# Gated-recurrence values and gates for two heads at a time, in a hybrid decoder block on one core

## The chip, the cores and the metric

The kernel runs on one core of a Trainium2 chip. The metric is the device time of the core in microseconds (us). Three runs of the kernel before gave 1631.12, 1628.74 and 1627.1 us, so the median is 1628.74 us.

Engine names: PE is the matrix engine (PEld its weight loads), DVE the vector engine, ACT the scalar engine, POOL the GpSimd engine, SP the engine whose queue issues most DMAs. Each engine takes its instructions in the order in which the program lists them, and waits where a semaphore holds the next one back.

## The reference, cut to what matters

One decoder block: x is (1, 1024, 1024) float32. A gated linear recurrence with four heads (HGRN2) and a sparse attention with eight heads are merged by gates; a squared-ReLU MLP of width 4096 follows.

```python
xn = rmsnorm(h, norm1_g)
proj = xn @ w_in
a_q, a_f, a_i, a_g, b_q, b_kv, b_gate, m_gate = split(proj)     # a_*: 4 heads x 128
y_a = hgrn2_mixer(a_q, a_f, a_i, a_g, lb, hgrn_norm_g)          # a_i: values, a_g: output gate
y_b = nsa_mixer(rope(b_q), ...)                                 # kc, vc: compressed keys and values
g_a, g_b = split(sigmoid(m_gate))
h = h + (g_a * (y_a @ w_br_a) + g_b * (y_b @ w_br_b)) @ w_out
hn = rmsnorm(h, norm2_g)
h = h + square(relu(hn @ w_ff1)) @ w_ff2
return rmsnorm(h, final_g)

# in hgrn2_mixer, by chunks of 64 tokens, for each head:
f = lb + (1 - lb) * sigmoid(f_pre); b = cumsum(log f)
o = tril(q e^b (k e^-b)^T) v + (q e^b) S                        # S: state ahead of the chunk
S = e^(b_last) S + (k e^(b_last - b))^T v
o = rmsnorm(o, norm_g) * silu(g)

# in nsa_mixer: compressed keys (and values alike)
blocks = tok[:, blk_idx] + pe                                   # 63 blocks of 32 tokens
kc = gelu(flatten(blocks) @ w1) @ w2                            # w1: 2048 x 256, w2: 256 x 64
```

## The kernel before

**Products.** A float32 product is made from three matmuls (`mm3`, lines 241 to 244): each operand is split into a rounded part (`whi`, `xh`) and a rest (`wlo`, `xl`). Weights come through a stream `W` (class `Stream`, line 119): SP loads a tile `wraw` of 512 KB, ACT casts it to `whi` (line 152), and DVE, or POOL for every third tile, subtracts to get `wlo` (line 155). The stream loads a set number of tiles ahead of use and splits fewer; the order of its entries is fixed by the `add_...` calls at lines 170 to 216.

**What sets the order.** The program is written out by hand, with generators for work that runs beside the main line. `spawn` starts a generator, `pump(ns)` in the main line advances a clock by `ns` and lets a generator whose due time has come take its next piece, and `drain` runs a generator to its end on the spot, with nothing of the main line between its pieces. A `yield 5000.0` in a generator asks for a pause of 5000 ns by that clock.

**Main line, in order.**

- To 44 us: `proj_vg(0)`: x comes in, is normalised, transposed (`pt`, `xh`, `xl`), and the values and gates of head 0 are made in 128x256 matmuls (`pv`).
- 44 to 290 us: `proj_f`, `proj_q` (tiles `gT`, 128x512 matmuls) and `proj_vg` for heads 1 to 3; the recurrence of the head before (`hgrn(h)`, line 451) runs beside them. It works in two halves, each with state updates on DVE (`S`, lines 507 to 512), outputs `po`, a normalisation (ACT, POOL, DVE, `h` at line 534) and transposes `py` (line 540).
- To about 400 us: gates `m` and the branch product `z` (`pz`), and the 280-column product for keys, values and the attention's gates (`pp`).
- 400 to about 548 us: the eight gate tiles of branch B (`gT`, written to `gb_d`) and `proj_b(0)` (`pp`, `kvt`, `qt`), with `compress()` (line 621) beside them. For each of k and v, compress has tokens transposed (`ptk`, `tokS`), four sets of `fh` (8 ACT and 8 DVE instructions each, lines 657 and 658), 12 matmuls `ph` on each set with a tile of its own weight stream `C`, a gelu chain on `ct` (lines 670 to 678), transposes `pgl` (line 685), and a last small product `pc2`.
- 548 to about 900 us: `proj_b(1)` and attention; then merge and `w_out` to 992 us (`po`, `hx` at line 1408).
- From 992 us: the MLP. `norm2` (line 1116) normalises the rows of `hx`, the sums `hs` and `hn` are transposed (`pt`, line 1108), split (`xoh`, `xol`, line 1114) and used in the first MLP matmuls `f1a`. The MLP's weights are split into `w1op` by `f1_prep` (line 1200) through `split2` (line 1191). A generator-like helper `ahead` runs the next such splits.

Of the kernel before, what the change touches and what calls it, by code (L numbers as in the profile page):

```python
# [10 lines left out]
F32R = mybir.dt.float32r  # L11
# [9 lines left out]
NT = T // 128  # L21
# [33 lines left out]
def tile_hybrid_block(ctx, tc, x, positions, norm1_g, w_in, lb_param, hgrn_norm_g, pe_k, pe_v,  # L55
# [116 lines left out]
    def add_vg(h):  # L172
        for i in range(2):
            W.add([vg_w[:, i * 4:(i + 1) * 4, e, h * 128:(h + 1) * 128] for e in range(2)], (4, 256))
# [17 lines left out]
    for h in range(1, 4):  # L192
        add_f(h)
        add_q(h)
        add_vg(h)
    ZSEQ = []
    for ct in range(8):
        ZSEQ.append(("m", ct))
        if ct >= 2:
            ZSEQ.append(("z", ct - 2))  # L200
    ZSEQ += [("z", 6), ("z", 7)]
    for kind, ct in ZSEQ:
        if kind == "m":
            add_mg(ct)
        elif ct % 2 == 0:
            W.add(w_cols(w_br_a[0], ct * 128, 256, k=4), (4, 256))
    for k0, k in ((0, 3), (3, 3), (6, 2)):
        W.add([w_cols(w_in2, C_KV, 256, k0=k0, k=k), w_cols(w_in2, C_BG, 24, k0=k0, k=k)], (k, 280))
    for ct in range(8):
        add_mg(8 + ct)  # L210
# [15 lines left out]
    W.ensure(2, 0)  # L226
# [78 lines left out]
    def vg_pair(h, tp, wvg, prologue=False):  # L305
        pv = psB("pv")
        for e in range(2):
            t = tp * 2 + e
            if prologue:
                if t + 4 < NT:  # L310
                    load_x(t + 4)
                if t:
                    transposed(XN.pop(t), t, XT[t // 4])
                if t + 2 < NT:
                    norm1(t + 2)
                if t in (1, 2):
                    W.ensure(W.i + t, W.i + t)
            for kt in range(KT):
                w = wvg[kt // 4]
                mm3(pv[:, e * 256:(e + 1) * 256], X_st(kt, t), (w[0][:, kt % 4, :], w[1][:, kt % 4, :]),  # L320
                    kt == 0, kt == KT - 1)
            pump(2600)
        if tp % 2 == 0:
            VG[h, tp // 2] = s4(name="vg").rearrange("p (i t c) -> p i t c", i=2, t=4)
        vg = VG[h, tp // 2]
        nc.vector.tensor_copy(vg[:, :, (tp % 2) * 2:(tp % 2) * 2 + 2, :].rearrange("p i e c -> p e i c"),
                              pv.rearrange("p (e i c) -> p e i c", e=2, i=2))

    def proj_vg(h, prologue=False):
        if prologue:  # L330
            norm1(0)
            W.ahead = 0
        wvg = [W.get(), W.get()]
        if prologue:
            transposed(XN.pop(0), 0, XT[0])
            norm1(1)
            W.ahead = 2
        for tp in range(4):
            vg_pair(h, tp, wvg, prologue)
# [11 lines left out]
    proj_vg(0, prologue=True)  # L351
# [99 lines left out]
    def hgrn(h):  # L451
        S = None
        st = []
        for q4 in range(2):
# [81 lines left out]
            yield 5000.0  # L536
# [840 lines left out]
    for th in range(2):  # L1377
# [107 lines left out]
```

## Time and profile before

| what | value |
|---|---|
| median of three runs | 1628.74 us (1627.1 to 1631.12) |
| profiled execution | 1628.69 us, its span 1626.6 us |
| PE busy | 1599.6 us |
| mean granted clock of PE | 0.998 of full speed |
| DVE, ACT, POOL busy | 67%, 46%, 36% of the span |

The profile is of one execution, and 2.1 us of its time lie around the span. Busy time of PE counts matmuls from start to a modelled end; the step from one start to the next shows the pace. The list of waits gives, for PE, each line that waited, the instruction that ended the wait, and the total. The chain of waits that ended last is 91% PE. The timeline lists instructions in order of start; in brackets stands the idle time of the engine just before the instruction, and what ended it.

### The profile page before, as it was taken

Reading aid. Unit: us, or ns where it says so; the run is one execution under the profiler, and the core shown is the slowest. Engines: PE = TensorE matmul, PEld = TensorE weight load, DVE = VectorE, ACT = ScalarE, POOL = GpSimd, SP = SyncE. Lnnn points to the kernel's source line nnn. Section 1 sums busy time; section 2 is a strip of 40 time slices with the busy share of each in tenths; the row PEclk is TensorE's granted clock in tenths of the full one; section 3 lists DMA queues with packets and bytes.
Section 4 is the critical chain, followed back from the end, with each engine's and each line's share of the span. In section 5 each row is a group of like instructions: output and inputs, shape, how many; then the busy total and the mean of one; then the engine's idle time right before and its main releaser. Section 6 shows DMA issues by size and latency. Waiting matters only on the chain.

```text
span 1626.6 us, 22947 instructions
## 1 busy us (share of the span) xinstructions
PE 1599.6 (98%) x8342; PEld 1339.9 (82%) x8342; DVE 1085.2 (67%) x1635; ACT 742.9 (46%) x1422; POOL 579.1 (36%) x567
## 2 busy tenths in 40 slices
PE   8999999999999999999999998999999999999998
PEld 7898898889888888788878877888888888888886
DVE  6464354122537466988887557988888868888766
ACT  5343335230646365877764324433333446333443
POOL 2222222010112354444341124455555303664554
PEclk9999999999999999999999999999999999999999
DMA  6211111232425000000027832344444599988852
GB/s 189 73 38 29 39 40 26 89 95 91 133 91 172 27 1 1 1 2 1 2 71 281 277 109 81 127 156 155 143 148 151 192 331 324 313 298 319 296 188 104
DMA packets 145827, 211.67 MB, mean 130 GB/s; under 512 B 11649, under 2 KB 72241, under 8 KB 145714
## 3 DMA queue, kind: packets, MB, share of 16 engines
q1 hardware_dynamic: 145714, 210.21, 38.3%
q8 instruction: 66, 1.08, 0.3%
q14 instruction: 47, 0.39, 0.1%
HBM read 164.03 MB, written 46.14 MB: 129 GB/s over the span
## 4 chain that ended last, share of the span: by engine, by line
PE 91%; DVE 3%; ACT 3%; issue 1%; DMA 1%; POOL 1%; POOLq 0%; SPq 0%; ACTq 0%; DVEq 0%
PE f1c L1226 8%; PE f1d L1226 5%; PE gT L242 5%; PE gT L244 5%; PE gT L243 5%; PE f1a L1226 5%; PE oT L1045 5%; PE sc L894 4%; PE pT L934 4%; PE gA L243 3%; PE gA L244 3%; PE gA L242 3%; PE gB L242 3%; PE gB L243 3%; PE gB L244 3%; PE pp L242 2%
## 5 line engine op out<-in xcount | busy, mean ns | idle before, releaser
L1314 POOL TENSOR_TENSOR gr<-gw 128x512 f32<-128x512 f32 x80 | 126.4, 1591 | 134.3 <-DVE gu L1195 50.7
L155 POOL TENSOR_TENSOR wlo<-wraw,whi 128x1024 fp32r<-128x1024 f32 (+1 forms) x28 | 67.4, 2407 | 273.9 <-ACT whi L152 269.6
L242 PE MATMUL gT<-xh,whi 128*128 128x512 f32 x384 | 152.6, 398 | 0.2 <-ACT xh L263 0.2
L244 PE MATMUL gT<-xh,wlo 128*128 128x512 f32 x384 | 150.3, 392 | 0.0
L243 PE MATMUL gT<-xl,whi 128*128 128x512 f32 x384 | 150.2, 391 | 0.0
L155 DVE TENSOR_TENSOR wlo<-wraw,whi 128x1024 fp32r<-128x1024 f32 (+2 forms) x59 | 81.9, 1395 | 93.5 <-ACT whi L152 89.0
L919 POOL TENSOR_SCALAR P<-P,den,gat 128x640 f32<-128x640 f32 (+7 forms) x128 | 100.1, 797 | 120.2 <-DVE den L915 61.4
L1195 DVE TENSOR_TENSOR gu<-gr,gu 128x512 fp32r<-128x512 f32 x112 | 103.0, 920 | 48.3 <-ACT gu L1194 48.1
L1194 ACT CAST gu<-gr 128x512 fp32r<-128x512 f32 x112 | 69.4, 620 | 136.9 <-DVE gx L1195 107.5
L1226 PE MATMUL f1c<-xoh,w1op 128*128 128x512 f32 x384 | 126.1, 390 | 0.0
L1195 DVE TENSOR_TENSOR gx<-gr,gx 128x512 fp32r<-128x512 f32 x112 | 111.1, 992 | 4.4 <-ACT gx L1194 4.2
L937 DVE TENSOR_TENSOR pth<-pT,pth 128x512 fp32r<-128x512 f32 (+1 forms) x148 | 98.8, 683 | 21.3 <-ACT pth L936 19.9
L910 ACT ACTIVATE P<-sc,den 128x640 f32<-128x640 f32 (+7 forms) x128 | 89.7, 705 | 43.9 <-DVE den L901 40.6
L894 PE MATMUL sc<-kS,qS 128*128 128x512 f32 (+3 forms) x384 | 96.7, 361 | 0.6 <-ACT P L910 0.5
L1045 PE MATMUL oT<-pth,vS 128*128 128x512 f32 x264 | 96.7, 441 | 0.0
L936 ACT CAST pth<-pT 128x512 fp32r<-128x512 f32 (+1 forms) x148 | 85.1, 588 | 23.9 <-PE pT L934 21.3
L901 DVE TENSOR_REDUCE den<-sc 128x1 f32<-128x640 f32 (+7 forms) x96 | 84.6, 884 | 16.7 <-PE sc L897 15.9
L152 ACT CAST whi<-wraw 128x1024 fp32r<-128x1024 f32 (+2 forms) x87 | 88.6, 1038 | 12.1 <-PE po L243 6.1
L243 PE MATMUL gA<-gx,gu 128*128 128x512 f32 x224 | 87.4, 390 | 0.4 <-DVE gx L1195 0.2
L242 PE MATMUL gA<-gx,gu 128*128 128x512 f32 x224 | 87.3, 390 | 0.0
L244 PE MATMUL gA<-gx,gu 128*128 128x512 f32 x224 | 87.2, 389 | 0.0
L242 PE MATMUL gB<-gx,gu 128*128 128x512 f32 x224 | 87.1, 389 | 0.0
(343 smaller groups left out, 4450.2 us busy)
## 6 DMA issues: line engine op xcount, KB each, us to landing
gw<-in_w_ff_dram SPq DMA_DIRECT2D x160, 256.0 KB, 5.3
gr<-u_d SPq DMA_DIRECT2D x112, 256.0 KB, 5.2
wraw<-in_w_in_dram SPq DMA_DIRECT2D x40, 512.0 KB, 5.1
w1r<-in_w_ff_dram SPq DMA_DIRECT2D x32, 512.0 KB, 4.5
wraw<-in_w_out_dram SPq DMA_DIRECT2D x16, 512.0 KB, 7.1
u_d<-ua SPq DMA_DIRECT2D x16, 512.0 KB, 2.8
u_d<-ub SPq DMA_DIRECT2D x16, 512.0 KB, 2.8
u_d<-uc SPq DMA_DIRECT2D x16, 512.0 KB, 2.8
```

What stands on the lines that cost most here:

```text
L155: eng.tensor_tensor(lo, raw, fb(hi), op=OP.subtract)
L242: nc.tensor.matmul(o, l[0], r[0], start=start, stop=False)
L243: nc.tensor.matmul(o, l[0], r[1], start=False, stop=False)
L244: nc.tensor.matmul(o, l[1], r[0], start=False, stop=stop)
L894: nc.tensor.matmul(sc[:, cs], qS[th][g][:, hh, qsl], kS[half][br][:, g * 2 + x_, ks], start=x_ == 0, stop=x_ == 1 and not masks)
L910: nc.scalar.activation(PP[qb, g, i], sv[:, hh - h0], AF.Exp, bias=den[:, 2, i:i + 1], accum_out=den[:, 0, i:i + 1])
L919: nc.gpsimd.tensor_scalar(pv_, pv_, den[:, 1, i:i + 1], gat[:, qb, (g * 4 + h_) * 3 + 1 + br:(g * 4 + h_) * 3 + 2 + br], op0=OP.mult, op1= ...
L937: nc.vector.tensor_tensor(pth[:n, 1], pt[:n], fb(pth[:n, 0]), op=OP.subtract)
L1045: nc.tensor.matmul(oT, vv, pth[:m, x_], start=i == 0 and x_ == 0, stop=i == n - 1 and x_ == 1)
L1195: nc.vector.tensor_tensor(l, src, fb(h), op=OP.subtract)
L1226: nc.tensor.matmul(dst, w_[:, kt, :], x_.kt(kt), start=first and kt == 0 and i == 0, stop=kt == 3 and i == 2, skip_group_check=True)
L1314: nc.gpsimd.tensor_tensor(t0[:, 1], t1[:, 0], t1[:, 1], op=OP.add if GORDER[i][1][2] > 0 else OP.subtract)
```

## The change

**Values and gates.** `vg_pair` becomes `vg_tile`: values and gates of two heads (0 and 1, later 2 and 3) are made together, one token tile at a time, in 128x512 matmuls. The weight tiles are (2, 512) instead of (4, 256), four for a pair of heads. Each `pv` is copied out by one DVE and one ACT instruction of 128x256, instead of one DVE instruction of 128x512 for two token tiles. At the start, four weight tiles instead of two are asked for ahead of x tiles 1 to 3.

**Order of heads and gates.** f0 q0 f1 q1, then values and gates of heads 2 and 3, then f2 q2 f3 q3. `hgrn(1)` starts in the middle of the second `proj_vg`, `hgrn(3)` after the second of five gate tiles of branch B that now stand ahead of the `m`/`z` sequence. `z` follows `m` by one step instead of two. Three gate tiles (5 to 7) are left beside `compress`.

**The pause before `py`** goes from 5000 to 6400.

**MLP weights.** `f1_prep` of parts (0, P1), (0, P2) is put ahead of the last `w_out` product but one, and that of (1, P1), (1, P2) into the first step of the last; they took place after the second step. The buffers that they use are given by number.

```diff
     def add_vg(h):
-        for i in range(2):
-            W.add([vg_w[:, i * 4:(i + 1) * 4, e, h * 128:(h + 1) * 128] for e in range(2)], (4, 256))
+        for i in range(4):
+            W.add([vg_w[:, i * 2:(i + 1) * 2, e, h * 128:(h + 2) * 128] for e in range(2)], (2, 512))
...
-        add_vg(h)
-    ZSEQ = []
+        if h == 1:
+            add_vg(2)
+    NB = 5
+    ZSEQ = [("b", 8 + ct) for ct in range(NB)]
     for ct in range(8):
         ZSEQ.append(("m", ct))
-        if ct >= 2:
-            ZSEQ.append(("z", ct - 2))
-    ZSEQ += [("z", 6), ("z", 7)]
+        if ct >= 1:
+            ZSEQ.append(("z", ct - 1))
+    ZSEQ.append(("z", 7))
...
-    for ct in range(8):
+    for ct in range(NB, 8):
         add_mg(8 + ct)
...
-    W.ensure(2, 0)
+    W.ensure(4, 0)
...
+    def vg_tile(h, t, wvg, prologue=False):
+
         pv = psB("pv")
...
+            if t in (2, 4):
+                W.ensure(W.i + t // 2, W.i + t // 2)
+        for kt in range(KT):
+            w = wvg[kt // 2]
+            mm3(pv, X_st(kt, t), (w[0][:, kt % 2, :], w[1][:, kt % 2, :]), kt == 0, kt == KT - 1)
+            if kt == 3:
+                pump(2600)
+        pump(2600)
+        pv4 = pv.rearrange("p (i e c) -> p i e c", i=2, e=2)
         for e in range(2):
...
+            if t % 4 == 0:
+                VG[h + e, t // 4] = s4(name="vg").rearrange("p (i t c) -> p i t c", i=2, t=4)
+            dst = VG[h + e, t // 4][:, :, t % 4, :]
+            if e:
+                nc.scalar.copy(dst, pv4[:, :, e, :])
+            else:
+                nc.vector.tensor_copy(dst, pv4[:, :, e, :])
...
-            yield 5000.0
+            yield 6400.0
             py = psB("py")
...
-    for h in range(1, 4):
-        proj_f(h)
-        proj_q(h)
-        proj_vg(h)
+    proj_f(1)
+    proj_q(1)
+    for _ in proj_vg(2):
         drain(hg)
-        hg = spawn(hgrn(h))
+        hg = spawn(hgrn(1))
+    proj_f(2)
+    proj_q(2)
+    drain(hg)
+    hg = spawn(hgrn(2))
+    proj_f(3)
+    proj_q(3)
...
+        if kind == "b":
+            gate_b(ct - 8)
+            if ct == 9:
+                drain(hg)
+                hg = spawn(hgrn(3))
+            continue
...
     cmp_ = spawn(compress())
-    for ct in range(8):
-        pg = gemm_T(W.get())
-        gb = s4(name="gb")
-        sigmoid(gb, pg, gb)
-        nc.sync.dma_start(gb_d[ct * 128:(ct + 1) * 128, :], gb)
+    for ct in range(NB, 8):
+        gate_b(ct)
...
-        FOP[p, nm] = split2(W1S[p][FW[nm]], ring("w1op", 5, n_op[0], F32R), 4)
+        FOP[p, nm] = split2(W1S[p][FW[nm]], ring("w1op", 5, n_op[0] if i is None else i, F32R), 4)
...
                 f1_load(0)
                 f1_sums(0)
+                f1_prep(0, "P1", 0)
+                f1_prep(0, "P2", 2)
...
-                    if j == 1:
-                        ahead(-1)
+                    if j == 0:
+                        f1_prep(1, "P1", 1)
+                        f1_prep(1, "P2", 3)
+                        n_prep[0] = n_op[0] = 4
```

What this makes of the order of instructions, at three places. Line numbers of the changed kernel stand some lines further down (L242 is L244 there, L155 has not moved).

On PE, at the end of the compress branch for v (last `ph`, then `pgl`, then the last product `pc`), before:

```order
L244 MATMUL ph<-whi,fh 126x256
L244 MATMUL pp<-whi,xl 128x512
L242 MATMUL pp<-whi,xh 128x512
...
L244 MATMUL pp<-whi,xl 128x512
L685 MATMUL pgl<-ident,ct 128x126 x2
L242 MATMUL pp<-whi,xh 128x512
...
L244 MATMUL pp<-whi,xl 128x512
L699 MATMUL pc_4330<-ct 63x64 x4
L242 MATMUL pp<-whi,xh 128x512
```

and in the changed kernel:

```order
L246 MATMUL ph<-whi,fh 126x256
L712 MATMUL pgl<-ident,ct 128x126 x2
L726 MATMUL pc_4179<-ct 63x64 x4
L244 MATMUL pp<-whi,xh 128x512
L245 MATMUL pp<-wlo,xh 128x512
```

Before, 28 `pp` matmuls stand between the last `ph` and `pgl`, and 12 between `pgl` and `pc`; in the changed kernel none stands at either place. Of the four sets of 12 `ph` for v, the last three stand one behind the other, where before `pp` and `gT` matmuls stood between all of them.

On DVE, the gelu chain of the same place (`ct`; `wlo` belongs to the weight stream, `rtmp` and `qt` to the rotary step of the queries), before:

```order
L155 TENSOR_TENSOR wlo<-wraw,whi 128x1024
L671 TENSOR_TENSOR ct<-ct 126x256
L672 TENSOR_SCALAR ct<-ct 126x256
L673 TENSOR_TENSOR ct<-ct 126x256
L674 TENSOR_SCALAR ct<-ct 126x256
L676 TENSOR_SCALAR ct<-ct 126x256
L677 RECIPROCAL ct<-ct 126x256
L678 TENSOR_TENSOR ct<-ct 126x256
L687 COPY ct<-pgl 128x252
```

and in the changed kernel:

```order
L700 TENSOR_TENSOR ct<-ct 126x256
L155 TENSOR_TENSOR wlo<-wraw,whi 128x1024
L701 TENSOR_SCALAR ct<-ct 126x256
L703 TENSOR_SCALAR ct<-ct 126x256
L704 RECIPROCAL ct<-ct 126x256
L155 TENSOR_TENSOR wlo<-wraw,whi 128x1024
L705 TENSOR_TENSOR ct<-ct 126x256
L773 TENSOR_TENSOR rtmp<-qt,trig 128x128
L774 TENSOR_TENSOR rtmp<-qt,trig 128x128
...
L777 TENSOR_TENSOR qt<-qt,rtmp 128x16x8
L714 COPY ct<-pgl 128x252
```

Two `wlo` moved into the chain, and five steps of the rotary step (two that are left out read like the others) moved ahead of the copy of `pgl`.

On DVE, where the MLP begins (`hx` is the residual, `hn`, `hs` the normalised rows and their sums), before:

```order
L1123 SCALAR_TENSOR_TENSOR hn<-hx,st,grow 128x1024
L1195 TENSOR_TENSOR w1op<-w1r,w1op 128x512 x4
L1408 TENSOR_TENSOR hx<-hx,po 128x512
L1140 TENSOR_TENSOR hs_9160<-hn 128x512 x2
L1141 TENSOR_TENSOR hn<-hn 128x512
L1123 SCALAR_TENSOR_TENSOR hn<-hx,st,grow 128x1024
L1142 TENSOR_TENSOR hn<-hs_9160,hn 128x512
L1141 TENSOR_TENSOR hn<-hn 128x512
L1142 TENSOR_TENSOR hn<-hs_9160,hn 128x512
L1408 TENSOR_TENSOR hx<-hx,po 128x512
L1140 TENSOR_TENSOR hs_9209<-hn 128x512
L1141 TENSOR_TENSOR hn<-hn 128x512
```

and in the changed kernel:

```order
L1147 SCALAR_TENSOR_TENSOR hn<-hx,st,grow 128x1024
L1219 TENSOR_TENSOR w1op<-w1r,w1op 128x512 x2
L1434 TENSOR_TENSOR hx<-hx,po 128x512
L1164 TENSOR_TENSOR hs_8792<-hn 128x512
L1165 TENSOR_TENSOR hn<-hn 128x512
L1147 SCALAR_TENSOR_TENSOR hn<-hx,st,grow 128x1024
...
L1434 TENSOR_TENSOR hx<-hx,po 128x512
L1147 SCALAR_TENSOR_TENSOR hn<-hx,st,grow 128x1024
L1434 TENSOR_TENSOR hx<-hx,po 128x512
L1164 TENSOR_TENSOR hs_8841<-hn 128x512
```

Two of the four `w1op` splits went to the start of the product before, the other two stand ahead of the second of the last four `hx` steps instead of the third, and the last two `hx` steps have one `hn` step between them instead of seven steps of the norm.

## Rows read from the trace of the kernel before

**Rows 1.** Page, busy time: us, share of the span, number of instructions.

```profile
PE 1599.6 (98%) x8342; PEld 1339.9 (82%) x8342; DVE 1085.2 (67%) x1635; ACT 742.9 (46%) x1422; POOL 579.1 (36%) x567
```

**Rows 2.** Waits of PE: line waited for, total us, times, longest us.

```profile
PE pt L1108 <- DVE xol L1114: 4.6, 2, 4.0
PE py L540 <- DVE h L534: 4.2, 4, 1.1
PE pgb L239 <- DVE evod L446: 2.4, 1, 2.4
PE pt L260 <- DVE xn L303: 1.9, 1, 1.9
...
PE ph L242 <- ACT whi L152: 0.5, 1, 0.5
```

**Rows 3.** Timeline, PE: start us, duration us, instruction; two runs of matmuls.

```profile
35.85 0.28 PE L243 MATMUL pv<-wlo,xh 128*128 128x256 f32 x1
...
38.49 0.28 PE L244 MATMUL pv<-whi,xl 128*128 128x256 f32 x1
...
125.55 0.39 PE L242 MATMUL gT<-xh,whi 128*128 128x512 f32 x1
...
128.97 0.39 PE L242 MATMUL gT<-xh,whi 128*128 128x512 f32 x1
```

**Rows 4.** Timeline, PE, around one head's output transposes.

```profile
120.77 0.49 PE L524 MATMUL po<-S,h 128*128 128x128 f32 x2
...
124.37 0.30 PE L540 MATMUL py<-ident,h 128*128 128x128 f32 x1 [1.02 <-DVE h L534]
```

**Rows 5.** Timeline, DVE: first and third of a run of state updates.

```profile
140.06 0.35 DVE L512 SCALAR_TENSOR_TENSOR S<-pkv,ec,S 128x128 f32<-128x128 f32 x1
...
141.87 0.35 DVE L512 SCALAR_TENSOR_TENSOR S<-pkv,ec,S 128x128 f32<-128x128 f32 x1
```

**Rows 6.** Page, costliest groups: busy us, mean ns, idle before; weight splits.

```profile
L155 POOL TENSOR_TENSOR wlo<-wraw,whi 128x1024 fp32r<-128x1024 f32 (+1 forms) x28 | 67.4, 2407 | 273.9 <-ACT whi L152 269.6
...
L155 DVE TENSOR_TENSOR wlo<-wraw,whi 128x1024 fp32r<-128x1024 f32 (+2 forms) x59 | 81.9, 1395 | 93.5 <-ACT whi L152 89.0
...
L152 ACT CAST whi<-wraw 128x1024 fp32r<-128x1024 f32 (+2 forms) x87 | 88.6, 1038 | 12.1 <-PE po L243 6.1
```

**Rows 7.** Timeline, all engines, end of the compress branch.

```profile
507.60 2.48 ACT L657 ACTIVATE fh<-tokS,cols 128x63 fp32r<-128x63 f32 x8
...
511.05 1.23 DVE L155 TENSOR_TENSOR wlo<-wraw,whi 128x1024 fp32r<-128x1024 f32 x1 [0.26 <-ACT whi L152]
...
513.63 0.28 PE L244 MATMUL ph<-whi,fh 128*126 128x256 f32 x1
...
513.94 0.37 ACT L670 COPY ct<-ph 126x256 f32<-126x256 f32 x1 [1.17 <-PE ph L244]
...
518.49 0.42 DVE L678 TENSOR_TENSOR ct<-ct 126x256 f32<-126x256 f32 x1
...
520.52 0.42 DVE L687 COPY ct<-pgl 128x252 f32<-128x252 f32 x1 [1.61 <-PE pgl L685]
```

**Rows 8.** Timeline, DVE: second and sixth step of the rotary step.

```profile
548.11 0.28 DVE L750 TENSOR_TENSOR rtmp<-qt,trig 128x128 f32<-128x128 f32 x1
...
548.92 0.28 DVE L754 TENSOR_TENSOR qt<-qt,rtmp 128x128 f32<-128x128 f32 x1
```

**Rows 9.** Timeline, DVE and PE, where the MLP begins.

```profile
985.11 2.49 DVE L1195 TENSOR_TENSOR w1op<-w1r,w1op 128x512 fp32r<-128x512 f32 x4
...
994.83 0.67 DVE L1408 TENSOR_TENSOR hx<-hx,po 128x512 f32<-128x512 f32 x1
...
1003.41 0.66 PE L1108 MATMUL pt<-ident,hn 128*128 128x128 f32 x4 [4.04 <-DVE xol L1114]
```

**Rows 10.** Windows: us, busy of PE, PEld, DVE, ACT, POOL, granted clock, DMA.

```profile
999.00:1003.40 4.40, 0.36 (x2) 0.00 (x0) 4.40 (x7) 1.19 (x3) 1.64 (x1) 1.00 0.00 0
1003.40:1008.00 4.60, 4.59 (x17) 3.70 (x18) 4.60 (x6) 1.18 (x2) 3.97 (x3) 0.63 0.00 0
```

More of the change, by code (lines that the diff above doesn't have):

```diff
@@ L194, in tile_hybrid_block @@
         add_q(h)
-        add_vg(h)
-    ZSEQ = []
+        if h == 1:
+            add_vg(2)
+    NB = 5
+    ZSEQ = [("b", 8 + ct) for ct in range(NB)]
     for ct in range(8):
         ZSEQ.append(("m", ct))
-        if ct >= 2:
-            ZSEQ.append(("z", ct - 2))
-    ZSEQ += [("z", 6), ("z", 7)]
+        if ct >= 1:
+            ZSEQ.append(("z", ct - 1))
+    ZSEQ.append(("z", 7))
     for kind, ct in ZSEQ:
-        if kind == "m":
+        if kind in "mb":
             add_mg(ct)
@@ L303, in norm1 @@
         nc.vector.scalar_tensor_tensor(XN[t], xt, rs, pgb, op0=OP.mult, op1=OP.mult)
-    def vg_pair(h, tp, wvg, prologue=False):
+    def vg_tile(h, t, wvg, prologue=False):
         pv = psB("pv")
-        for e in range(2):
[L308 to L327, printed above, removed]
+        if prologue:
+            if t + 4 < NT:
+                load_x(t + 4)
+            if t:
+                transposed(XN.pop(t), t, XT[t // 4])
+            if t + 2 < NT:
+                norm1(t + 2)
+            if t in (2, 4):
[7 more added lines that the diff above has]
+        pv4 = pv.rearrange("p (i e c) -> p i e c", i=2, e=2)
+        for e in range(2):
+            if t % 4 == 0:
[5 more added lines that the diff above has]
+                nc.vector.tensor_copy(dst, pv4[:, :, e, :])
     def proj_vg(h, prologue=False):
@@ L332, in proj_vg @@
             W.ahead = 0
-        wvg = [W.get(), W.get()]
+        wvg = [W.get() for _ in range(4)]
         if prologue:
@@ L337, in proj_vg @@
             W.ahead = 2
-        for tp in range(4):
-            vg_pair(h, tp, wvg, prologue)
+        for t in range(NT):
+            vg_tile(h, t, wvg, prologue)
+            if not prologue and t == 3:
+                yield
     def proj_f(h):
@@ L349, in proj_q @@
         nc.scalar.copy(Q[h], pq)
-    proj_vg(0, prologue=True)
+    for _ in proj_vg(0, prologue=True):
+        pass
     hng = attc.tile([128, 128], F32)
@@ L560, in tile_hybrid_block, with gate_b @@
     GA = {}
-    for kind, ct in ZSEQ:
+    def gate_b(ct):
+        pg = gemm_T(W.get())
+        gb = s4(name="gb")
+        sigmoid(gb, pg, gb)
+        nc.sync.dma_start(gb_d[ct * 128:(ct + 1) * 128, :], gb)
+    for kind, ct in ZSEQ:
+        if kind == "b":
[4 more added lines that the diff above has]
+            continue
         if kind == "m":
@@ L565, in tile_hybrid_block @@
             sigmoid(GA[ct], pg, GA[ct])
-            if ct == 2:
+            if ct == 0:
                 drain(hg)
@@ L1198, in tile_hybrid_block, with f1_prep @@
     n_op = [0]
-    def f1_prep(p, nm):
+    def f1_prep(p, nm, i=None):
         if nm == FORDER[4 if p < 2 else 3] and p < NP - 1:
             f1_sums(p + 1)
-        FOP[p, nm] = split2(W1S[p][FW[nm]], ring("w1op", 5, n_op[0], F32R), 4)
+        FOP[p, nm] = split2(W1S[p][FW[nm]], ring("w1op", 5, n_op[0] if i is None else i, F32R), 4)
         n_op[0] += 1
```

## The prediction

> **What bounds the kernel now.** I read the busy times first: PE is busy 1599.6 us of a span of 1626.6 [rows 1], so 27 us of idle time are all that can be won by removing waits, and any new idle time of PE is paid in full. Then the list of waits of PE [rows 2]: the largest items are 4.6 us at the start of the MLP, 4.2 us at the recurrence's output transposes `py` (four waits of about 1.05) and 4.3 us in the prologue (`pgb` and `pt`). The compress branch, which the change also touches, costs PE only 0.5 us today. The reader is to see that the change can win a few us at each place, and that it takes cover away at a place which today has almost no idle time.
>
> About 0.3% of this kernel, 4.9 us, is what a measurement can tell from no change; "faster" and "slower" below mean more than that. The sum is made against the profiled execution, 1628.69 us, which agrees with the median of 1628.74.
>
> **Wider matmuls for values and gates.** 768 matmuls of 128x256 become 384 of 128x512. The narrow ones step by (38.49 - 35.85)/22 = 0.120 us, the wide ones by (128.97 - 125.55)/15 = 0.228 [rows 3]. So each pair saves 0.012, and the whole 384 x 0.012 = 4.6 us, all on PE's path since PE bounds this stage. The copies out of `pv` go half to ACT; both engines have room there, so they cost nothing unless PE waits for a `pv` buffer. The Trainium skill (TensorE: Matmul & The Clock Gate, Back-to-back issue gap) gives 262 cycles for 256 columns and 518 for 512, which is 6 cycles or 2.5 ns for a pair; by that the gain would be an estimated 1.0 us, and the forecast 3.6 us later. The trace does not bear it out: its pair saves 12 ns.
>
> **Prologue.** Four weight tiles of the same 512 KB instead of two go ahead of x tiles 1 to 3, and the first tile of matmuls now lasts twice as long, which gives the next x tile more time. I take 0.7 us of gain; the bounds are the gain of the whole `pt` wait, 1.9, and a loss of the same size if x comes late [rows 2].
>
> **The pause before `py`.** Today four of the eight halves have 9 `gT` matmuls (9 x 0.228 = 2.05 us) between the last `po` and the first `py`, where the normalisation needs about 3.1 us: `po` ends at about 121.3, `py` starts at 124.37 after 1.02 of idle time [rows 4]. In the new order two halves have 17 (3.9 us, enough), and two still have 9. So half of 4.2 goes: 2.1 us gained. Bounds: 0 (a wait on another step of the same chain) and 4.2.
>
> **State updates.** In the second halves only 12 wide `gT` matmuls (2.7 us) stand between the products that feed `S` and the `po` that reads it; today 48 narrow ones (5.8 us) stand there in the halves beside `pv`. The update takes about 2.2 us from its first step to the end of its third [rows 5], and nearly fits. In head 0, DVE has decay steps of the next half queued in between. I take 1 us of loss, from 0 (ready in time) to 2.5 (the whole update exposed).
>
> **The compress branch, the term that decides.** Five of the eight gate tiles moved ahead, so three are left beside compress, and its last part no longer fits under them and `proj_b(0)`. It is drained: the last three `ph` sets stand back to back on PE, then `pgl` and the last product, with nothing between. PE must then wait for the chain that feeds them. I count from the first matmul of the last `pp` tile before it (0):
>
> - ACT makes a set of `fh` in 2.48 us [rows 7] and casts a weight tile in 1.04; the rest `wlo` takes 2.4 on POOL and 1.4 on average on DVE [rows 6], and 1.23 there at this place [rows 7], which I use. A set of 12 `ph` takes 12 x 0.12 = 1.4.
> - ACT starts at 0.6: `fh` 1 done at 3.1, `fh` 2 at 5.5, cast at 6.5, `wlo` on POOL at 8.95. PE has done 18 `pp`, set 1 and 6 `pp` by 6.9: it waits 2.1 and ends set 2 at 10.3.
> - `fh` 3, the copy of `qt` and the cast end at 10.4, `wlo` on DVE at 11.7: PE waits 1.3, set 3 ends at 13.1.
> - `fh` 4 ends at 12.9, the cast at 13.9, `wlo` at 15.2: PE waits 2.1, set 4 ends at 16.6. Sum of the three waits: 5.4 us.
> - The gelu chain takes 5.0 us today, from 513.94 to 518.91, under 28 `pp` matmuls [rows 7]. In the new order PE has nothing for it, and DVE has two `wlo` of 1.2 inside the chain: 5.0 + 2.45 = 7.45 us. After `pgl`, five steps of the rotary step (0.2 each, from (548.92 - 548.11)/4 [rows 8]) stand ahead of the copy of 0.42 [rows 7], so another 1.25 us or so until the last product: 8.7 us.
>
> Together 14 us. Bounds: at least 6 (the chain without any insertion, plus the copy; that PE has no other matmul there is set by the order), at most 18 (each `wlo` 1.4 to 2.4 us, as where DVE and POOL work side by side). To this comes the clock. After the 4.04 us wait at the MLP's start PE ran the next 4.6 us at a granted clock of 0.63, a mix of both levels, 1.2 and 2.4 GHz [rows 9, 10]; that cost about 2 us. The wait for the gelu chain is longer, so I add 2 us (0 to 4).
>
> What `ph` waits for is queued in order: behind `fh` on ACT stand the weight stream's casts and the copy of `qt`; behind the gelu chain on DVE stand the rotary steps of queries and keys, which attention needs. The stall delays all alike. SP's queue holds the weight loads: they wait for `pp` matmuls that are done early, so I take them to have landed.
>
> **MLP operands.** Today four `w1op` splits (2.49 us from 985.11) delay the last two `hx` steps, the last of which starts at 994.83, some 3 us after PE has gone on to the MLP; PE then waits 4.04 us for `xol` [rows 9]. In the new order two splits are done during the product before, two stand one `hx` step earlier, and I get the last `hx` at about 992.6, 2.3 us earlier. PE's wait shrinks to about 2.0, and part of the slow clock behind it goes, with some new small waits of under 1 us later. I take 3.5 us of gain; the bounds are 0 (another step is late) and 6.6 (the list's 4.6 and 2 of slow clock).
>
> **Sum.** -4.6 - 0.7 - 2.1 + 1 + 14 + 2 - 3.5 = +6.1. The forecast is 1628.7 + 6.1 = 1634.8 us, 0.4% slower, just beyond the 4.9.
>
> **Rivals.**
>
> *Compress costs little (faster).* Mechanism: ACT runs ahead of PE at the drained sets, so that they wait for nothing, and no `wlo` delays the gelu chain. It decides if ACT starts the first `fh` set some 5.4 us before the last `pp` tile's first matmul. For it: ACT is busy 46% and may be early. Against it: `fh` needs `tokS`, whose last transposes stand only 30 `pp` matmuls (6.8 us) ahead of the first `ph`, and ACT must do 13 us of sets and casts. The price falls to 6 us with no slow clock, while the gains are 10.9: 1628.7 - 10.9 + 1 + 6 = 1624.8; with the whole 6.6 at the MLP, 1621.7. Chance 0.17, of which a little lies within 4.9 us.
>
> *Half the price (no change).* The waits for `ph` halve, one `wlo` less stands in the way and the clock holds: 10 us in all. 1628.7 - 9.9 + 10 = about 1629. Chance 0.26.
>
> *The MLP's start doesn't move, or the stall is at its upper bound (slower still).* The change then does not do what it says at `xol`: another DVE step is last, the 3.5 us do not come, and the time is 1638.3; with 18 us and a clock loss of 4 instead of 16 together it would be 1640.8. Chance 0.13.
>
> The forecast's own case, 1630 to 1638, has the remaining 0.44. Most of it, 0.37, lies beyond 1633.6, 0.07 below.
>
> **How the numbers follow.** Slower: 0.37 + 0.13 = 0.50. Within 0.3%: 0.26 + 0.07 + 0.03 of the first rival = 0.36. Faster: 0.14. The range takes in the two middle cases whole, and the outer ones in part: from 1623.5, where the first rival is cut, to 1641, the upper bound of the stall.
>
> **What would show each step.** `pv` steps of 0.228 us, and some 4 to 5 us less up to the end of the recurrence. In the list of waits `py` falls to about 2 us. New lines for `ph` (about 5 us, on `wlo` of DVE and POOL), `pgl` (about 7, on DVE `ct`) and the last product (about 1.2): if they sum to under 8, the term that decides was wrong, and the kernel is not slower. A granted clock clearly below 1 in the slice around 500 to 540 us. The `pt` wait at the MLP falls to about 2; if it stays at 4, that term was wrong. The forecast fails most simply if ACT gets through `fh` before PE arrives.

## The result and the profile after

The changed kernel takes 1646.38 us (median of four runs, 1645.26 to 1649.18); before took 1627.92 beside it. The ratio is 1.0112, with a 95% interval of 1.0098 to 1.0126: 1.1% slower, where 0.4% was forecast and 1641 was the upper end of the range. The profiled execution took 1646.24 us, with a span of 1644.2, 17.6 more than before.

Busy time of the changed kernel (page; us, share, instructions), beside [rows 1]:

```profile
PE 1597.8 (97%) x7958; PEld 1319.1 (80%) x7958; DVE 1088.7 (66%) x1635; ACT 748.1 (46%) x1438; POOL 580.2 (35%) x567
```

PE has 1.8 us less work than before and 19.4 us more idle time. Its list of waits (line waited for, what ended the wait, total us, times, longest), beside [rows 2]:

```profile
PE pgl L712 <- DVE ct L705: 9.3, 1, 9.3
PE pv L246 <- DVE xl L266: 5.9, 2, 5.7
PE py L549 <- DVE h L543: 4.5, 4, 1.2
PE pt L1132 <- DVE xol L1138: 3.3, 2, 2.5
...
PE ph L245 <- DVE wlo L155: 2.1, 2, 1.1
PE ph L245 <- POOL wlo L155: 1.8, 1, 1.8
...
PE ph L244 <- ACT whi L152: 1.1, 2, 0.9
PE po L533 <- DVE S L516: 0.9, 3, 0.4
...
PE pc L726 <- DVE ct L714: 0.7, 1, 0.7
```

`py` and `pt` still stand there. New are `pgl`, `pc` and all of `ph` but the 0.9 of one earlier set (14.1 us together), the 5.9 us at `pv`, and 0.9 at `po`.

To see where time went, the program is cut at four marks that both kernels have: the start of the 288th matmul of `pv` and `gT` (end of `proj_q(0)`), of the first 128x280 product, of the first `ptq` (start of attention's preparation), and of the first `f1a` (MLP). Moved work is taken out at the pace of [rows 3]: 0.120 us for a narrow matmul, 0.228 for a wide one, and 10.9 us for a gate tile of 48 wide ones.

| stage | before | changed | work moved | excess |
|---|---|---|---|---|
| prologue, f0, q0 | 67.72 | 93.89 | +20.7 | +5.4 |
| recurrence, gates, m/z | 306.07 | 337.34 | +29.2 | +2.1 |
| compress, `proj_b(0)` | 183.64 | 147.94 | -54.5 | +18.8 |
| attention, merge, `w_out` | 434.34 | 434.34 | 0 | 0.0 |
| MLP to the end | 634.86 | 630.67 | 0 | -4.2 |

The moved work sums to -4.6, which is the gain of the wide matmuls if these paces hold; the excess sums to +22.1; together +17.5, the 17.6 of the span but for rounding. The forecast had -0.7, -1.1, +16, 0 and -3.5 in the column of excess.

**Compress.** The drained tail is as forecast: 4.1 us at `ph` (5.4 forecast), 9.25 at `pgl` (7.45), 0.7 at `pc` (1.25), 14.1 in all (14). The parts were off by -1.3, +1.8 and -0.5, so that the sum came out so close is in part luck. The last step of the gelu chain shows why `pgl` waited longer (timeline; start us, duration us, engine, instruction, in brackets the idle time before it and its releaser):

```profile
560.25 1.16 DVE L155 TENSOR_TENSOR wlo<-wraw,whi 128x1024 fp32r<-128x1024 f32 x1
561.33 2.56 DVE L705 TENSOR_TENSOR ct<-ct 126x256 f32<-126x256 f32 x1
...
560.17 3.43 POOL L155 TENSOR_TENSOR wlo<-wraw,whi 128x1024 fp32r<-128x1024 f32 x1 [12.95 <-ACT whi L152]
...
564.03 0.65 PE L712 MATMUL pgl<-ident,ct 126*128 126x126 f32 x2 [9.25 <-DVE ct L705]
```

`ct` at L705, 0.42 us long in [rows 7], took 2.56 beside a `wlo` on POOL, and ended 0.3 us after it (last section). The clock cost more than the 2 us that I gave it. Windows (us, busy of PE, PEld, DVE, ACT, POOL, granted clock, DMA share, GB/s):

```profile
540.00:554.00 14.00, 9.86 (x61) 8.30 (x60) 12.23 (x33) 11.85 (x34) 2.36 (x1) 1.00 0.61 178
554.00:564.00 10.00, 0.78 (x7) 0.57 (x6) 8.20 (x10) 3.61 (x5) 3.43 (x1) 0.67 0.07 27
564.00:572.00 8.00, 7.25 (x29) 5.94 (x30) 4.31 (x17) 1.64 (x4) 0.00 (x0) 0.55 0.01 2
572.00:580.00 8.00, 8.00 (x54) 6.96 (x52) 3.61 (x8) 4.06 (x10) 0.00 (x0) 1.00 0.00 0
```

The granted clock was still 1.00 while PE waited at `ph` (to 554 us) and fell within the long wait at `pgl`. From about 564 to 571 us, PE ran at about half speed, which is the level of 1.2 GHz: some 3.5 us lost. PE's waits in this stage rose by 14.5 us (the 14.1, and 0.9 at the earlier `ph` against 0.5 before), so 4.3 of the 18.8 are left, of which the slow stretch is the most.

**Prologue.** DMAs on SP, then DVE, then PE:

```profile
8.58 8.40 SPq L142 DMA_DIRECT2D wraw<-in_w_in_dram  x4
17.02 1.68 SPq L115 DMA_DIRECT2D xt<-in_x_dram  x1
...
19.25 0.33 SPq L372 DMA_DIRECT2D posi<-in_positions_dram  x1
...
24.26 0.21 DVE L374 CAST posf<-posi 8x128 f32<-8x128 int32 x1 [5.98 <-DMA posi<-in_positions_dram]
24.40 1.27 DVE L266 TENSOR_TENSOR xl<-pt,xh 128x512 fp32r<-128x512 f32 x2
...
25.12 0.80 PE L246 MATMUL pv<-whi,xl 128*128 128x512 f32 x1 [5.73 <-DVE xl L266]
25.72 0.63 PE L244 MATMUL pv<-whi,xh 128*128 128x512 f32 x1
```

`posf`, the cast of the positions, waited 5.98 us on DVE for a load of 4 KB that SP issued at 19.25 us, behind 2 MB of weights. `xl`, which PE needed, stood behind it. PE idled 5.73 us at 25.12, and the next matmuls stepped by 0.43 us instead of 0.228. In the kernel before, the same cast waited too, but stood behind the `xl` of that token tile in DVE's order:

```profile
18.67 1.89 DVE L264 TENSOR_TENSOR xl<-pt,xh 128x512 fp32r<-128x512 f32 x3 [0.56 <-ACT xh L263]
23.32 0.21 DVE L365 CAST posf<-posi 8x128 f32<-8x128 int32 x1 [2.76 <-DMA posi<-in_positions_dram]
```

**Recurrence.** The four `py` waits are still 4.5 us. ACT and PE at the second half of head 2:

```profile
257.22 0.27 ACT L538 ACTIVATE h<-po 128x128 f32<-128x128 f32 x1
...
257.46 1.06 ACT L293 ACTIVATE gb<-gb 128x1024 f32<-128x1024 f32 x1
258.41 0.28 ACT L538 ACTIVATE h<-po 128x128 f32<-128x128 f32 x1
...
261.20 0.30 PE L549 MATMUL py<-ident,h 128*128 128x128 f32 x1 [1.18 <-DVE h L543]
```

Between `po` and `py` there are now 17 `gT` matmuls, as I had read, but ACT ran the passes of a gate tile (`gb`, 1.06 us each) between the steps of the normalisation, which needs 5.0 us here instead of 3.1. The wait is as long as before.

**MLP.** The longest `pt` wait fell from 4.04 to 2.51, and no slow stretch follows (compare [rows 9, 10]):

```profile
1022.75 0.66 PE L1132 MATMUL pt<-ident,hn 128*128 128x128 f32 x4 [2.51 <-DVE xol L1138]
...
1021.00:1026.00 5.00, 3.25 (x18) 2.78 (x19) 5.00 (x8) 1.18 (x2) 2.62 (x2) 1.00 0.00 0
```

### The profile page after: what moved, and what is told of

Its sections match the earlier page's. It is cut to its first block, busy times and chain, and to the rows that moved or that the text cites. A ratio compares the mean times of both kernels' runs of the same rounds, so it can differ in the third digit from the quotient of the medians.

```text
span 1644.2 us, 22198 instructions
## 1 busy us (share of the span) xinstructions
PE 1597.8 (97%) x7958; PEld 1319.1 (80%) x7958; DVE 1088.7 (66%) x1635; ACT 748.1 (46%) x1438; POOL 580.2 (35%) x567
## 4 chain that ended last, share of the span: by engine, by line
PE 86%; ACT 4%; DVE 4%; issue 2%; DMA 1%; SPq 1%; POOL 1%; POOLq 0%; DVEq 0%; ACTq 0%
PE f1c L1250 8%; PE f1d L1250 5%; PE f1a L1250 5%; PE gT L246 5%; PE gT L244 5%; PE gT L245 5%; PE oT L1069 4%; PE sc L918 4%; PE pT L958 4%; PE gA L245 3%; PE gA L246 3%; PE gA L244 3%; PE gB L244 3%; PE gB L246 3%; PE gB L245 3%; PE pp L244 2%
## 5 line engine op out<-in xcount | busy, mean ns | idle before, releaser
L155 POOL TENSOR_TENSOR wlo<-wraw,whi 128x1024 fp32r<-128x1024 f32 (+1 forms) x28 | 68.0, 2430 | 309.5 <-ACT whi L152 280.5
L155 DVE TENSOR_TENSOR wlo<-wraw,whi 128x1024 fp32r<-128x1024 f32 (+1 forms) x59 | 80.9, 1374 | 113.2 <-ACT whi L152 110.9
L244 PE MATMUL gT<-xh,whi 128*128 128x512 f32 x384 | 152.6, 397 | 0.0
L152 ACT CAST whi<-wraw 128x1024 fp32r<-128x1024 f32 (+1 forms) x87 | 88.7, 1037 | 14.8 <-PE po L245 6.1
L244 PE MATMUL gA<-gx,gu 128*128 128x512 f32 x224 | 87.3, 390 | 0.0
```

The source lines that it names most:

```text
L155: eng.tensor_tensor(lo, raw, fb(hi), op=OP.subtract)
L244: nc.tensor.matmul(o, l[0], r[0], start=start, stop=False)
```

## The experiments

Each run is compared with before on the same chip (median 1628 to 1630 us). "Excess" is the last column of the table above, worked out in the same way from the one profiled execution of each run.

**The cast later.** The positions are cast into another tile, which moves the cast 20 instructions down in DVE's order, to 54.23 us (a planner turns the written program into each engine's order, so an edit of this kind can move an instruction).

```diff
-    posf = attc.tile([8, 128], F32)
+    posf = cs4[:8, 896:1024]
```

> The changed kernel with one edit: the cast of the positions (posf) writes into the setup tile, so that it stands 14 rows later in DVE's order; all loads keep their places. Theory A (the cast waits 5.98 us on DVE for a small load and holds back xl of the second token tile): PE's wait of 5.73 us at pv goes, with most of the 1.6 us that the slow clock cost behind it; the time falls by 5 to 7 us, to about 1640. Theory B (x tiles 1 to 3 come late because four weight tiles stand ahead of them on SP): PE waits in the same place or at the next pt for x instead, and the time falls by less than 2 us.

1646.96 us, ratio 1.0111 [1.0094, 1.0128]: no gain. The wait at the second token tile is gone, but the third now waits (ACT, then PE):

```profile
23.86 1.06 ACT L250 ACTIVATE xn<-xt 128x1024 f32<-128x1024 f32 x1 [3.01 <-DMA xt<-in_x_dram]
...
27.95 1.05 ACT L265 CAST xh<-pt 128x512 fp32r<-128x512 f32 x2
...
28.56 0.50 PE L244 MATMUL pv<-whi,xh 128*128 128x512 f32 x1 [2.82 <-ACT xh L265]
...
31.09 0.79 PE L246 MATMUL pv<-whi,xl 128*128 128x512 f32 x1 [1.79 <-DVE xl L266]
```

ACT's square for x4 waited for its load until 23.86 us; three squares and a cast later comes `xh`, at 27.95, and PE waits 2.8 and 1.8 us. Theory A was right about the first wait and wrong about the price: a second instruction in an in-order queue waited for a transfer behind the same 2 MB, and it took the whole gain.

**Two weight tiles ahead of x, as before.**

```diff
-    W.ensure(4, 0)
+    W.ensure(2, 0)
```

> The changed kernel with two weight tiles instead of four asked for ahead of x tiles 1 to 3, as before. In DVE's order the cast of the positions then stands behind both xl of the second token tile instead of ahead of them. Theory A: the wait of 5.7 us at pv goes; PE waits instead up to 2 us at the start for the third and fourth weight tile; 1640 to 1642. Theory B: x comes in time, no wait at pv or pt beyond 1 us: 1639 to 1640, with x3 landed by 16 us instead of 23.9.

1644.12 us in the one run, slower than both theories said; the excess of the prologue falls from 5.4 to 3.8. The wait at `pv` for `xl` is down to 1.3 us, but PE waits for weights at the start and some waits at `pt` and `pv` remain. So the doubled weight load at the start is at most a part of it: the granted clock stayed at 1.00 there in this execution, and the seven slow steps had cost the changed kernel some 1.5 us.

**All x tiles ahead of the f and q weights, and the late cast.**

```diff
-            W.ahead = 0
+            W.load, W.ahead = 0, 0
...
-            W.ahead = 2
+            W.load, W.ahead = 4, 2
...
-    posf = attc.tile([8, 128], F32)
+    posf = cs4[:8, 896:1024]
```

> The changed kernel with two edits in the prologue: the late cast of the positions as in the run of that name, and no weight tiles for the gates f and q loaded until x tiles 4 to 6 have been issued (the read-ahead of the stream is 0 until then). The theory after the first runs: two things are queued in order behind late transfers, the cast on DVE (posi) and the squares on ACT (x4, behind 2 MB of f and q weights on SP, landed at 23.9 us); taking away only one lets the other end the wait. With both gone the stretch up to the end of proj_q(0) falls by 4.5 to 7 us and PE's waits at pv and pt between 18 and 33 us sum to under 1.5 us: 1639.5 to 1642. Rival (DVE and ACT work of the prologue is the bound with two heads at a time): less than 2 us, with waits left on xl or xh while no DMA is waited for.

1641.63 us (1639.39 to 1642.26), ratio 1.0078 [1.0059, 1.0097]: some 5 us less than the changed kernel. The excess of the prologue is 0.2 us instead of 5.4. Between 18 and 33 us, PE's waits at `pv` and `pt` sum to 0.5 us (under 1.5 expected). In the list of waits one item is left at `pv`, the longest part of it ahead of that stretch, at 11.4 us; the stage as a whole stands where the moved work puts it:

```profile
PE pv L244 <- ACT xh L265: 2.4, 4, 1.7
```

So the prologue's loss is the order of loads on SP together with two instructions, one on DVE and one on ACT, that wait at the head of their queues. The one on ACT alone is enough to keep it (the run with the late cast); x first without the later cast was not run.

**Two gate tiles ahead of m/z instead of five.**

```diff
-    NB = 5
+    NB = 2
...
-        if ct >= 1:
-            ZSEQ.append(("z", ct - 1))
-    ZSEQ.append(("z", 7))
+        if ct >= 2:
+            ZSEQ.append(("z", ct - 2))
+    ZSEQ += [("z", 6), ("z", 7)]
...
-            if ct == 0:
+            if ct == 2:
                 drain(hg)
```

> The changed kernel with two gate tiles instead of five ahead of the m/z sequence, z two steps behind m, and the last head drained at m 2, as before; six gate tiles stay beside compress. PE's order then has 30 pp matmuls between the last ph and pgl, and pp between all ph sets. If the drained compress tail is what costs 18 to 19 us there (14.1 us of waits on ph, pgl and the last product, and about 4 us of slow clock), these waits fall below 1.5 us, the granted clock stays at 1.0 there, and the time falls by 16 to 19 us, to 1627 to 1630. Rival (the gates ahead of m/z hide something worth as much in the recurrence): new waits at py or S of 5 us or more come back, and the time falls by less than 12 us.

1639.58 us, ratio 1.0066 [1.0051, 1.0081]: 7 us less than the changed kernel, not 16 to 19. The waits at `ph`, `pgl` and `pc` are gone, and others have come (PE's waits, then POOL):

```profile
PE ptk L665 <- POOL tok L660: 4.5, 2, 3.7
...
PE po L533 <- DVE S L516: 2.9, 4, 2.0
...
PE pa L494 <- DVE h L485: 2.0, 1, 2.0
...
508.58 2.36 POOL L155 TENSOR_TENSOR wlo<-wraw,whi 128x1024 fp32r<-128x1024 f32 x1 [8.54 <-ACT whi L152]
510.91 2.17 POOL L660 TENSOR_SCALAR tok<-kct 128x512 f32<-128x512 f32 x2
```

The excess of compress fell from 18.8 to 6.0; PE's waits make 4.0 of it, which is `ptk` (4.5) less the 0.5 of before. PE's `ptk` waits for `tok` on POOL behind a `wlo` that waited 8.5 us for its cast on ACT. The recurrence's excess rose from 2.1 to 6.7, since head 3 has a gate tile less beside it (`S` 2.0 us at its second half, `pa` 2.0). In the profiled execution 1.7 us more were lost where the MLP begins, where the slow clock came back (below, at the MLP edit). Theory and rival were both half right.

**Both together.** The two diffs above.

> The prologue edits of the run before and two gate tiles instead of five ahead of m/z together. If the two places are independent, the gains add up: 5 to 6 us of the prologue and the 7 us of the two-gate run, 1633 to 1635; still not faster than the kernel before by the waits left at ptk (4.5 us), S and pa (4 us). Rival (the POOL wait at ptk was a consequence of the prologue's shift of the stream's every-third-tile rule): below 1630.

1636.71 us, ratio 1.0047 [1.0029, 1.0064]. The excess is -0.1, 6.7 and 7.1 in the first three stages: the two places add up, with the `ptk`, `S` and `pa` waits unchanged. The time lies 1.7 us above what was expected; in the profiled execution the stage up to the MLP took 1.6 us more than in the changed kernel, by the clock (last section).

**Three gate tiles ahead, head 3 with four beside it, x first.** As above with NB = 3.

> The prologue edits (late cast, x first) with three gate tiles ahead of m/z, z two steps behind m and head 3 drained at m 2: head 3 keeps four gate tiles beside it as in the changed kernel, and five stay beside compress, so that 30 pp matmuls stand between the last ph and pgl, and only the last product stands right behind pgl. If the losses are the three found (prologue 5.4, recurrence 2.1 with all its cover, drained compress tail 18.8), the prologue loss goes, the recurrence stays at 2, compress costs 1 to 5 (the last product's 1.3, some POOL wait at ptk) and the gains of 4.6 (wide matmuls) and 4.1 (MLP) show: 1622 to 1629. Rival (five gate tiles are too few beside compress however they stand, since its casts and splits are late): waits at ph or ptk of more than 6 us and 1632 or more.

1634.85 us (1631.87 to 1637.84), ratio 1.0027 [1.0017, 1.0036]: the rival's time, though not its waits. The recurrence has its cover again (excess 2.2), but compress has an excess of 11.3, in spite of 30 `pp` matmuls between the last `ph` and `pgl` (`issue`: the list names nothing that ended the wait; DVE's and POOL's rows of that time follow):

```profile
PE pc L726 <- issue: 2.6, 1, 2.6
...
PE pgl L712 <- DVE ct L705: 2.4, 2, 1.6
PE ph L245 <- DVE wlo L155: 2.0, 1, 2.0
...
552.03 2.46 DVE L774 TENSOR_TENSOR rtmp<-qt,trig 128x128 f32<-128x128 f32 x1
554.51 0.42 DVE L714 COPY ct<-pgl 128x252 f32<-128x252 f32 x1
...
552.00 2.34 POOL L155 TENSOR_TENSOR wlo<-wraw,whi 128x1024 fp32r<-128x1024 f32 x1 [9.40 <-ACT whi L152]
```

The wait at `pc` has the same look as the changed kernel's `pgl`: a step on DVE, 0.28 us long in [rows 8], took 2.46 beside a `wlo` on POOL, and the copy that `pc` reads stood behind it. Of the 11.3, PE's waits make 6.7; most of the rest is slow clock (granted 0.51 from 553 to 560 us). The prologue, with the edits of the two runs before, has an excess of 2.0 here, with 3.2 us of waits at `pv`, so the gain there varies from run to run.

So in these runs the excess of compress goes with the number of gate tiles left beside it: 8 tiles 0, 6 tiles 6.0 and 7.1, 5 tiles 11.3, 3 tiles 18.8, which is 3.0 to 3.8 us for each tile taken away. Which wait shows (`ptk`, `ph`, `pgl`, `pc`) changes from run to run; that some shows doesn't.

**The gelu of v left out.**

```diff
+            if kv == 0:
-            nc.vector.tensor_tensor(u, hx, hx, op=OP.mult)
+                nc.vector.tensor_tensor(u, hx, hx, op=OP.mult)
...
```

> The changed kernel without the eight instructions of the gelu between the copy of ph and pgl for v (left out; the k half keeps it). PE's order at the drained tail is unchanged: 36 ph, pgl, last product back to back. If the 9.25 us wait of pgl is the exposed chain, it falls to about 1 to 2 us (the ACT copy and at most one interposed wlo), and if the slow clock of some 8 us behind it is the consequence of that wait, the granted clock stays near 1.0 there: 8 us less for the wait and 3 to 4 us for the clock, 1634 to 1636. Rival (the clock falls because of the ph waits ahead, or PE finds the weight splits of the next product late anyway): 4 to 8 us less only, with the waits moved to pc or pp.

1637.4 us in the one run, 9 us less than the changed kernel. The excess of compress falls by 10.8, from 18.8 to 8.0. The `pgl` wait falls from 9.25 to 0.46, those at the drained `ph` sets from 4.1 to 2.6, and the clock falls and recovers earlier (PE's wait, then windows as above):

```profile
PE pgl L713 <- ACT ct L697: 0.5, 1, 0.5
...
544.00:558.00 14.00, 10.40 (x55) 8.79 (x54) 9.67 (x22) 9.46 (x24) 2.36 (x1) 0.76 0.52 155
558.00:566.00 8.00, 8.00 (x48) 6.82 (x48) 6.22 (x14) 3.62 (x7) 2.39 (x1) 1.00 0.01 3
```

PE's waits in this stage fall from 15.0 to 4.3 us in all. That is nearly the whole of the 10.8, and the exposed chain is 8.8 of it; hardly anything came back from the clock. Here it fell behind the first `ph` wait of 1.8 us (granted 0.76 from 544 to 558 us), where the changed kernel, behind a wait of the same length at the same place, still had 1.00, and PE was busy about as long at the low level (6.0 us against 6.3). So the clock did not stay near 1.0 as the theory asked, and the rival is right that `ph` waits can lower it; they did not in the changed kernel's own profile.

**Gate passes left out.**

```diff
-        sigmoid(gb, pg, gb)
+        if ct < NB:
+            nc.scalar.copy(gb, pg)
+        else:
+            sigmoid(gb, pg, gb)
...
-            sigmoid(GA[ct], pg, GA[ct])
+            if ct:
+                sigmoid(GA[ct], pg, GA[ct])
+            else:
+                nc.scalar.copy(GA[ct], pg)
```

> The changed kernel with the sigmoid (three ACT passes of 1.05 us) of the five gate tiles ahead of m/z and of the first m tile left out (one copy in its place). The order then puts 9 gT instead of 17 between the last po and the first py in the second halves of heads 2 and 3. Theory (the number of gT there follows the length that the order's planner gives to the normalisation, and the wait is what the chip takes longer than that): py starts about 3.1 us after po instead of 5.0, and the four waits stay at 1.0 to 1.2 us each, 4.2 to 4.6 in all. Rival (the 17 matmuls are a cover of fixed size, used up by the ACT passes): with ACT free, py waits 2 us or more less in all, or not at all at these two places.

The time, 1654.97 us in the one run, is 9 us above the changed kernel. By stages, 2.6 of them lie in the prologue, which the edit doesn't touch, 2.8 in the recurrence, 2.4 from attention to `w_out` and 1.8 in the MLP, less 0.8 in compress; in the recurrence, `w_out` and the MLP the granted clock fell to 0.50 for a stretch where it was 1.00 in the changed kernel. By the trace, 9 `gT` stand again at both places, and the four waits are 1.00, 1.10, 2.51 and 1.10 us (PE, then POOL at the third):

```profile
PE py L549 <- DVE h L543: 5.7, 4, 2.5
...
258.98 2.38 POOL L155 TENSOR_TENSOR wlo<-wraw,whi 128x1024 fp32r<-128x1024 f32 x1 [7.39 <-ACT whi L152]
261.44 0.19 POOL L539 TENSOR_SCALAR ss<-ss 128x4 f32<-128x4 f32 x1
```

Three of four agree with the theory: the matmuls ahead of `py` follow the length that the order's planner gives to the normalisation, 9 for a chain of 3.1 us and 17 for one of 5.0, and a wait of about 1.1 us is left either way. At the one of 2.51 the normalisation's step on POOL (`ss`) stood behind a `wlo` until 261.4 us, some 1.5 us after ACT had done its part.

**The MLP edit alone, in the kernel before.**

```diff
                 f1_load(0)
                 f1_sums(0)
+                f1_prep(0, "P1", 0)
+                f1_prep(0, "P2", 2)
...
-                    if j == 1:
-                        ahead(-1)
+                    if j == 0:
+                        f1_prep(1, "P1", 1)
+                        f1_prep(1, "P2", 3)
+                        n_prep[0] = n_op[0] = 4
```

> The kernel before with the MLP edit alone (the four w1op splits earlier, with given buffers). If the 4.1 us between the start of the MLP and the end in the changed kernel come from this edit: 3.5 to 4.5 us faster than before, about 1624, with the pt wait at 2 to 2.5 instead of 4.0. Rival (the gain comes from another place in the MLP that the shifted order changes): less than 1.5 us.

1626.39 us, ratio 0.9984 [0.9975, 0.9993]: 2.6 us faster. In the profiled execution, 4.2 us are gained from the start of the MLP on, the same as in the changed kernel; 1.6 were lost in the stage before, by the clock (last section). The 4.2 isn't firm: of eleven profiled executions with this edit, nine gain 4.1 to 4.2 there and two (two gate tiles, gate copies) 2.4 to 2.5, with the slow clock back behind the `pt` wait; and one without the edit (the next run) is itself 1.6 shorter there than before.

**The wide matmuls for heads 2 and 3 alone, in the kernel before.** Everything else stays; the products stand behind q2, half of them beside head 1's recurrence, half beside head 2's.

```diff
+    wvg = [W.get() for _ in range(4)]
+    for t in range(NT):
+        vg_tile(2, t, wvg)
+        if t == 3:
+            drain(hg)
+            hg = spawn(hgrn(2))
+    proj_f(3)
+    proj_q(3)
+    drain(hg)
+    hg = spawn(hgrn(3))
```

> The kernel before with the wide matmuls for heads 2 and 3 alone: prologue, head 1, all eight gate tiles beside compress, m/z sequence and MLP are those of before; the values and gates of heads 2 and 3 are made together behind q2, four token tiles beside head 1's recurrence, four beside head 2's. If the widening is worth 0.012 us a matmul, 192 wide ones save 2.3 us (1627 to 1628), and compress shows no wait above the 0.5 of before. Rival (the recurrence loses its cover when the products are moved, as in the changed kernel): new waits at S, pa or py of 2 us and more, no gain.

1627.47 us, ratio 0.9983 [0.9974, 0.9992]. The stage of the recurrence is 1.8 us shorter (2.3 expected), and compress is as before (-0.1). The next run repeats both (1.7 and 0.0).

**Both of these.**

> The run before plus the MLP edit. If the two are independent: 2.3 and 2.8 to 4.1 us, together 4.5 to 6.5 us less than before, 1623 to 1625, ratio 0.996 to 0.997. Rival: one takes the other's gain, 1626 to 1628.

1624.08 us (1622.70 to 1626.66), ratio 0.9964 [0.9951, 0.9976]: 5.9 us faster than before by the medians, and some 22 faster than the changed kernel. The two gains add up. Its `py` and `pt` waits:

```profile
PE py L565 <- DVE h L559: 4.3, 4, 1.2
PE pt L1145 <- DVE xol L1151: 3.3, 2, 2.5
```

## Why the prediction was wrong

The sign, the place and the price of the term that decides were right: the drained tail's waits were forecast at 14 us and measured at 14.1. The sum was 11.5 us short of the span's 17.6: 6.1 in the prologue, 3.2 in the recurrence, 2.8 in compress, less 0.7 at the MLP. The steps:

- **Prologue**, forecast -0.7 and measured +5.4: 6.1 us. The step that failed is "I take 0.7 us of gain", and its bounds of 1.9 to either side, which came from the waits of the kernel before. I looked at when x and the weights land, not at what stands ahead of `xl` and `xh` in DVE's and ACT's order. The positions' cast was one row of that order. The copies of `pv` on ACT, which I had costed at nothing, cost 0.9 more at a `pt`. The x-first edits took the loss away in two runs of three and left 2.0 in the third; the cast alone took none.
- **`py`**, forecast -2.1 and measured +0.3: 2.4 us. I took 17 matmuls as cover for a chain of 3.1 us. In the new order gate passes on ACT stretch the chain to 5.0. The same gate tiles that I counted as work moved are work on ACT at the place that they move to. A wait of 0.6 at `pv` for a `wlo` on POOL is also new there.
- **Slow clock behind the tail**, forecast 2 and measured 3.5 by the slow stretch, 4.3 as what the waits leave of the 18.8: the term was mis-sized by some 2 us, since I took the wait of 4.04 us as the pattern. Behind that one PE ran at 0.63 for 4.6 us, behind the 9.25 at 0.55 for 8.
- **The tail's waits**, forecast 14 and measured 14.1, by parts that were off to either side. One sum was off by its own rows: five rotary steps of 0.2 and a copy of 0.42 are 1.4, not 1.25; the wait was 0.7.
- **State updates**, forecast +1: 0.9 of waits at `po` for `S`. Right.
- **MLP**, forecast -3.5, measured -4.2, and the same with the edit alone, in one profile each. Right; the wait fell to 2.5 instead of 2.0, and more of the slow clock went.
- **Wide matmuls**, forecast -4.6. The table takes the 4.6 as given and doesn't test it; the run with half of them alone gave 1.8 of 2.3 in its stage. The Trainium skill (TensorE: Matmul & The Clock Gate, Back-to-back issue gap) would have given an estimated 0.5 us for that half; the measurement stands nearer to the rows.

The forecast's rival "compress costs little" asked that ACT run ahead at the drained sets, so that PE waits for nothing there; PE waited 14.1 us. Beyond the prediction, the runs say that the tail is only the visible end: taking two, three or five gate tiles from beside compress cost 3.0 to 3.8 us each, so that spreading the tail (two or three tiles ahead) lessened and moved the waits but did not end them. And the recurrence needs those tiles as well once head 1's products stand in the prologue. The change as a whole takes head 1's products, 23 us of narrow matmuls, out of the recurrence, fills the hole from compress, and loses there.

What stays open: the 2.6 us that the single run with gate copies lost in the prologue, why the start of the MLP differs by 1.6 us between executions of the same code, and whether the cost for each tile is that of the tile alone, since the order around it changed in each run too.

## What to carry to other kernels

Before work is moved ahead, list what it covers where it stands, and price the stage that loses it: a stage that shows almost no idle time may be one whose cover is exactly used up. For each wait that ought to go, read the whole queue of the engine that ends it, down to the smallest load and cast, since one row that waits at its head holds back all behind it, and taking one such row away may only show the next. The parts that pay without taking cover (here the earlier splits, and the wide matmuls of a late pair of heads) should be tried alone.

## What the runs showed of the hardware

A wait of the same length doesn't always lower the clock. At the start of `w_out`, all kernels wait 1.6 us and then 0.3 (0.5 with two gate tiles, 1.1 with the gate copies). In the kernel before, the window behind it (columns as above) reads

```profile
954.00:958.00 4.00, 4.00 (x20) 3.28 (x19) 2.75 (x2) 0.00 (x0) 3.90 (x3) 1.00 0.43 142
```

and in the run with the MLP edit alone

```profile
954.00:958.00 4.00, 4.00 (x13) 3.12 (x11) 3.91 (x3) 0.57 (x1) 3.57 (x3) 0.57 0.07 13
```

at the same place: granted clock 1.00 against 0.57, 20 matmuls started against 13, 1.6 us lost. Of the thirteen profiled executions, the stage from the first `po` to the first `f1a` takes 119.6 to 119.8 us in eight (before, changed, x first and wide pair alone among them), 121.1 to 121.2 in four (MLP edit alone, MLP edit with wide pair, x first with two tiles, no gelu of v), and 122.0 with the gate copies; the slow stretch stands in the last five alone. So 1.6 us of a difference between two single executions of this kernel can be the clock alone. The Trainium skill (TensorE: Matmul & The Clock Gate, HAM oscillation — how this bites in real kernels) describes a kernel whose waits for DMAs between bursts of matmuls, longer than 1.6 us, bring the clock down. These traces agree that a wait can do so, but here the shorter one did in five of thirteen executions.

An instruction on DVE can take six to nine times its time beside one on POOL: `ct` at L705 took 2.56 us with a POOL `wlo` running, 0.42 in [rows 7] without, and `rtmp` 2.46 in the run with three gate tiles, 0.28 in [rows 8]. Both began after the `wlo` and ended 0.15 to 0.3 us behind it, as if they had waited for its end; the `wlo` of 3.43 us, about 2.4 elsewhere, had itself run beside a DVE `wlo` of 1.16. Not every POOL instruction does this: in the run with two gate tiles the same `ct` took 0.42 beside POOL instructions of 128x128.
